# Gate-scaled one-hot matrices of the dense expert tiles: relu(gate - gate x distance) on ScalarE in place of a VectorE compare and a ScalarE scaling

## The chip, the cores and the metric

The kernel runs on one core of a Trainium2 chip. The metric is the device time of one execution in microseconds (us). A core has TensorE (PE in the profile; PEld is its weight load), VectorE (DVE), ScalarE (ACT), GpSimd (POOL) and SyncE (SP), each with its own queue of instructions that it works through in order, and DMA engines that all queues share.

## The reference

One layer of a decoder trunk on 1024 tokens of width 1024: a state-space branch, a dilated attention branch and a memory attention branch are merged and added to the residual, and then comes a retrieval of single-neuron experts. Only that last part matters here:

```
q = (hn @ w_query).reshape(b, s, 8, 2, 128)
sc = einsum('bshcd,hckd->bshck', q, sub_keys)
v1, i1 = top_k(sc[..., 0, :], 16);  v2, i2 = top_k(sc[..., 1, :], 16)
cand = v1[..., :, None] + v2[..., None, :]
cidx = i1[..., :, None] * 128 + i2[..., None, :]
top, pos = top_k(cand, 16);  idx = take(cidx, pos);  gate = softmax(top)
act = gelu(einsum('bld,blhkd->blhk', hn, expert_down[idx]))
out = einsum('blhk,blhkd->bld', gate * act, expert_up[idx])
```

There are 16384 experts; each token takes 8 x 16 = 128 of them, each with a gate.

## The kernel before

The sequence is worked through in two halves of four token tiles (128 tokens each). Of the eight tiles four (0, 1, 4, 5) gather their experts' rows by indirect DMA; the other four (2, 3, 6, 7, called DENSE) compute all 16384 experts and multiply each by its gate, which is zero for an expert that was not taken. For these a tile's gates have to be spread into a matrix "expert x token". `gates_of` does this: an expert number is `first * 128 + second`, and for each token a product of two one-hot matrices over its 128 slots, one from `second` (called `o2`) and one from `first` scaled by the gate (`og`), gives the 128x128 block of that token on TensorE.

`gates_of` begins with a set-up: it splits the expert numbers, transposes `first`, `second` and `gate` into one PSUM bank and copies them into `slots` (L1195). Then come 32 steps per tile, each for four tokens: a compare of `iota` with `second` (L1221), a compare of `iota` with `first` (L1222), both 128x512 on VectorE, four scalings of 128x128 on ScalarE (L1224), and, one step behind, `product()`: four matmuls of 128x128 (through the helper at L172, pinned in TensorE's program order) and a copy out of PSUM on ScalarE (L1207). After four steps a staging block is stored to `w_park` in device memory (L1210).

It runs in two places. For tiles 2 and 3 `early_gates` is a side job: `main()` steps it, by a counter of TensorE time, beside the attention and merging work of the second half; its one-hot matrices stand in the shared `work` buffers. For tiles 6 and 7 `dense` runs `gates()` together with `begin()`, which computes blocks of hidden activations (two 128x512 halves of weights loaded, cast on ScalarE at L244, the remainder on VectorE at L245, 24 matmuls, Gelu at L1266). There `hots` has room for four steps. Beside both run the side jobs of the gathered tiles: top-16 selection (`heads`), row products on VectorE (L1109, pinned) and the sums of rows on TensorE (L1154, pinned). After that the main loop of `dense` reads `w_park` back, so it begins when the last tile's blocks are stored.

The order of instructions on each engine is made when the program is built: by program order, readiness and the build's own cost estimates; pinned instructions keep their place, and weight casts in the mixing stages are moved ahead (`high_priority`).

Of the kernel before, what the change touches and what calls it, by code (L numbers as in the profile page):

```python
# [14 lines left out]
AF = mybir.ActivationFunctionType  # L15
ALU = mybir.AluOpType
# [86 lines left out]
def tile_hybrid_block(ctx: ExitStack, tc: tile.TileContext, keep_d, cst_d, vec_d, row_d, pos_d, xT_d, memT_d, w_in, w_mem_kv,  # L103
                      w_ssd_br, w_dil_br, w_mem_br, w_out, w_query, subk_d, down_d, up_d, downT_d, out):
    nc = tc.nc
# [44 lines left out]
    def gtiny(n, dt, tag, bufs):  # L150
        return new(gsmall, [P, n], dt, tag, bufs)[:, :n]
# [8 lines left out]
    def ps(tag=None):  # L160
        turn[0] += 1
        return bank(tag if tag and psums[tag][1] else "t" if turn[0] % 2 and psums["t"][1] else "s")
# [7 lines left out]
    def mm(o, lhsT, rhs, **kw):  # L170
        cost(o, 4 if rhs.dtype == F32 else 1)
        return nc.tensor.matmul(o, lhsT, rhs, **kw)  # L172

    def tr(o, x, i):
        cost(o, 2)
        nc.tensor.transpose(o, x, i)
# [6 lines left out]
    iota = keep[:, K_IOTA:K_IOTA + P]  # L183
# [914 lines left out]
    def pinned(ins):  # L1098

        tc.keep_in_program_order(ins)  # L1100
# [83 lines left out]
    def gates_of(d, expert, gate, alloc, ps, hot, stage_of):  # L1184

        t, slots = alloc(), alloc()
        ei = gtiny(P, I32, "ei", 1)
        nc.vector.tensor_copy(ei, expert)
        nc.vector.tensor_scalar(out=ei, in0=ei, scalar1=7, scalar2=None, op0=ALU.logical_shift_right)
        nc.vector.tensor_copy(t[:, 0:128], ei)  # L1190
        nc.vector.scalar_tensor_tensor(t[:, 128:256], t[:, 0:128], -128.0, expert, op0=ALU.mult, op1=ALU.add)
        tp = ps()
        for n, x in enumerate((t[:, 0:128], t[:, 128:256], gate)):
            tr(tp[:, n * P:(n + 1) * P], x, ident)
        nc.scalar.copy(slots[:, 0:384], tp[:, 0:384])  # L1195
        yield
        sl = slots[:, 0:384].rearrange("p (n t) -> p n t", n=3)
        iota4 = iota.unsqueeze(1).to_broadcast([P, 4, P])
        todo = []

        def product():
            (o2, og), stage, b, t4 = todo.pop(0)
            pw = ps()
            for tq in range(4):
                pinned(mm(pw[:, tq * P:(tq + 1) * P], o2[:, tq, :], og[:, tq, :], start=True, stop=True))
            for c0, n, part in stage:
                nc.scalar.copy(part[:, :, t4 * 4:t4 * 4 + 4], pw.rearrange("p (t c) -> p c t", t=4)[:, c0:c0 + n, :])  # L1207
            if t4 == WT // 4 - 1:
                for c0, n, part in stage:
                    nc.sync.dma_start(w_park[d * (P // WT) + b, :, c0:c0 + n, :], part)  # L1210

        for b in range(P // WT):
            stage = stage_of(b)
            for t4 in range(WT // 4):
                t0 = b * WT + t4 * 4

                def of(n):
                    return sl[:, n, t0:t0 + 4].unsqueeze(2).to_broadcast([P, 4, P])

                o2, og = (hot(n).rearrange("p (t c) -> p t c", t=4) for n in range(2))  # L1220
                nc.vector.tensor_tensor(out=o2, in0=iota4, in1=of(1), op=ALU.is_equal)  # L1221
                nc.vector.tensor_tensor(out=og, in0=iota4, in1=of(0), op=ALU.is_equal)  # L1222
                for tq in range(4):
                    nc.scalar.activation(out=og[:, tq, :], in_=og[:, tq, :], func=AF.Copy, scale=sl[:, 2, t0 + tq:t0 + tq + 1])  # L1224
                todo.append(((o2, og), stage, b, t4))
                if len(todo) == 2:
                    product()
                yield
        product()

    def dense(hn, dpool):
# [54 lines left out]
        def gates():  # L1286
            stages = new(dpool, [P, 2, P, WT], F32, "wbig", 2)
            hots = new(dpool, [P, 8, NW], F32, "wbig", 2)
            step = [0]

            def hot(n):
                step[0] += n == 0
                return hots[:, 2 * (step[0] % 4) + n, :]

            for d, tt in enumerate(DENSE):
                if tt >= NT:
                    while tt not in routed:
                        next(sides[-1][0])
                        yield
                    yield from gates_of(d, *routed[tt], dslab, big_ps, hot, lambda b: [(0, P, stages[:, b % 2])])  # L1300
# [92 lines left out]
    def early_gates():  # L1393
        def stage_of(b):
            return [(32 * k, 32, work().rearrange("p (c t) -> p c t", t=WT)) for k in range(4)]

        for d, tt in enumerate(DENSE):
            if tt < NT:
                while tt not in routed:
                    yield IDLE  # L1400
                for _ in gates_of(d, *routed[tt], work, ps, lambda n: work(), stage_of):
                    yield paces["gates"]
# [90 lines left out]
```

## Time and profile before

| what | value |
|---|---|
| runs of the kernel before | 4052.35 us median of 3 (4045.46 to 4067.32) |
| the profiled execution | 4053.3 us, span 4051.5 us |
| TensorE busy | 3770.0 us (93%) |
| VectorE busy | 2767.2 us (68%) |
| ScalarE busy | 1463.1 us (36%) |
| granted TensorE clock, mean | 0.960 |

The span is the time from the first to the last instruction of the profiled execution; the execution's own time is 1.8 us longer. Busy shares are over the whole span and mix stages with different limits. A granted clock of 1.0 is TensorE's full speed.

### The profile page before, as it was taken

The numbers are of one execution on the slowest core, as the hardware profiler recorded it, in microseconds if no ns is written. First come the engines' busy times: TensorE is split into PE (matmuls) and PEld (weight loads), VectorE is DVE, ScalarE is ACT, GpSimd is POOL, SyncE is SP. The second block draws the span as 40 slices with busy tenths as digits, with TensorE's granted clock in tenths as the row PEclk, the third lists the DMA queues.
The fourth block names the chain that finished last, engine by engine and source line by source line (L and its number), as shares of the span: only waits on it lengthen the run. The fifth ranks groups of instructions, "written<-read, shape, count | busy, mean of one in ns | idle before, by whom it ended". The sixth has DMA issues, their size and how long they took to land.

```text
span 4051.5 us, 54149 instructions
## 1 busy us (share of the span) xinstructions
PE 3770.0 (93%) x17838; PEld 2819.7 (70%) x17838; DVE 2767.2 (68%) x6987; ACT 1463.1 (36%) x3198; POOL 1424.6 (35%) x1257
## 2 busy tenths in 40 slices
PE   8989999999899998889888888999999999999997
PEld 5766888866676786667666676677777777777664
DVE  5763454558998768887768998976666666666432
ACT  3444344333333333445542564222223222222221
POOL 1210001101334433444345533444443344444444
PEclk9999999999999988989899999999999999999999
DMA  3233234443466757788788879989888888898888
GB/s 96 71 101 92 77 107 120 125 155 118 123 181 215 233 171 231 235 297 296 267 311 294 292 274 310 329 299 314 303 306 312 289 291 313 308 319 306 318 314 325
DMA packets 452826, 956.29 MB, mean 236 GB/s; under 512 B 44480, under 2 KB 173248, under 8 KB 450496
## 3 DMA queue, kind: packets, MB, share of 16 engines
q0 software_dynamic: 147456, 536.94, 38.0%
q1 hardware_dynamic: 305088, 415.90, 31.9%
q8 instruction: 140, 2.29, 0.2%
q14 instruction: 142, 1.16, 0.1%
HBM read 882.94 MB, written 69.73 MB: 235 GB/s over the span
## 4 chain that ended last, share of the span: by engine, by line
PE 31%; DMA 9%; DVE 8%; issue 4%; POOL 2%; ACT 1%; SPq 0%; POOLq 0%; another core or an unknown queue 0%; DVEq 0%; ACTq 0%
PE mm L172 15%; PE s L172 13%; DMA wraw<-in_downT_dram 4%; PE up L1154 4%; DVE wlo L245 1%; DMA wraw<-in_up_dram 1%; DVE rowd L1109 1%; DMA rowu<-in_up_dram,ids 1%; DMA rowd<-in_up_dram,ids 1%; POOL junk L1007 1%; POOL rowu L1168 1%; DVE wbig L1221 1%; DMA rowd<-in_down_dram,ids 1%; POOL rowd L1168 1%; DVE wbig L1222 1%
## 5 line engine op out<-in xcount | busy, mean ns | idle before, releaser
L245 DVE TENSOR_TENSOR wlo<-wraw,whi 128x512 fp32r<-128x512 f32 (+2 forms) x1002 | 714.0, 714 | 758.9 <-ACT whi L244 668.9
L244 ACT CAST whi<-wraw 128x512 fp32r<-128x512 f32 (+2 forms) x1002 | 612.7, 613 | 1704.7 <-PE mm L172 845.4
L1115 POOL DMA_INDIRECT rowd<-in_down_dram,ids x512 | 591.3, 1155 | 973.4 <-DVE act L1109 738.7
L172 PE MATMUL mm<-uslab,whi 128*128 128x512 f32 x2240 | 740.0, 409 | 6.2 <-DVE slab L427 5.9
L172 PE MATMUL s<-uslab,whi 128*128 128x512 f32 (+1 forms) x2080 | 667.2, 402 | 33.3 <-ACT whi L244 24.2
L172 PE MATMUL mm<-whi,coef 128*128 128x512 f32 x2048 | 677.4, 400 | 17.5 <-DVE acc L1345 10.7
L1109 DVE CUSTOM_DVE_ANT_0 rowd<-rowd,rowd 128x1024 f32<-128x1024 f32 x512 | 629.7, 1244 | 92.1 <-DMA rowd<-in_down_dram,ids 85.5
L1168 POOL DMA_INDIRECT rowu<-in_up_dram,ids x448 | 498.6, 1113 | 500.7 <-PE up L1154 380.0
L172 PEld LDWEIGHTS s<-uslab,whi 128*128 128x128 f32 (+1 forms) x2080 | 392.4, 191 | 161.2 <-ACT whi L244 34.2
L172 PEld LDWEIGHTS mm<-uslab,whi 128*128 128x128 f32 x2240 | 421.6, 193 | 99.1 <-issue 10.5
L172 PEld LDWEIGHTS mm<-whi,coef 128*128 128x128 f32 x2048 | 389.3, 190 | 142.8 <-issue 33.9
L172 PE MATMUL mm<-uslab,wlo 128*128 128x512 f32 x1120 | 454.0, 406 | 16.7 <-DVE wlo L245 16.6
L172 PE MATMUL s<-uslab,wlo 128*128 128x512 f32 (+1 forms) x1040 | 416.4, 400 | 11.1 <-DVE wlo L245 9.4
L172 PE MATMUL mm<-wlo,coef 128*128 128x512 f32 x1024 | 408.4, 399 | 2.2 <-DVE wlo L245 2.2
L172 PE MATMUL mm<-slab,whi 128*128 128x512 f32 x768 | 258.2, 415 | 18.3 <-DVE slab L245 6.2
L172 PEld LDWEIGHTS mm<-uslab,wlo 128*128 128x128 f32 x1120 | 215.4, 193 | 70.8 <-DVE wlo L245 21.1
L172 PEld LDWEIGHTS s<-uslab,wlo 128*128 128x128 f32 (+1 forms) x1040 | 198.3, 191 | 64.7 <-DVE wlo L245 17.3
L1154 PE MATMUL up<-rowu,one_col 128*32 128x512 f32 x1792 | 225.7, 611 | 18.8 <-DMA rowu<-in_up_dram,ids 18.8
L172 PE MATMUL mm<-whi,uslab 128*128 128x512 f32 (+1 forms) x768 | 240.4, 394 | 0.0
L1007 POOL TENSOR_TENSOR junk<-junk,code 128x800 f32<-128x800 f32 x64 | 129.6, 2025 | 294.7 <-DVE junk L1005 273.7
L172 PEld LDWEIGHTS mm<-wlo,coef 128*128 128x128 f32 x1024 | 194.9, 190 | 49.3 <-DVE wlo L245 4.5
L172 PEld LDWEIGHTS mm<-slab,whi 128*128 128x128 f32 x768 | 147.3, 196 | 56.5 <-DVE slab L245 8.9
(315 smaller groups left out, 5077.0 us busy)
## 6 DMA issues: line engine op xcount, KB each, us to landing
wraw<-in_downT_dram SPq DMA_DIRECT2D x256, 256.0 KB
wraw<-in_up_dram SPq DMA_DIRECT2D x256, 256.0 KB
wraw<-in_w_in_dram SPq DMA_DIRECT2D x152, 256.0 KB
wbig<-w_park SPq DMA_DIRECT2D x16, 2048.0 KB
wraw<-in_w_in_dram SPq DMA_DIRECT2D x160, 128.0 KB
slab<-y_park SPq DMA_DIRECT2D x64, 256.0 KB
wraw<-in_w_query_dram SPq DMA_DIRECT2D x64, 256.0 KB
w_park<-work SPq DMA_DIRECT2D x64, 256.0 KB
```

The lines of the kernel that those rows point to most:

```text
L172: return nc.tensor.matmul(o, lhsT, rhs, **kw)
L244: nc.scalar.copy(hi, src)
L245: nc.vector.tensor_tensor(out=lo, in0=src, in1=hi.bitcast(F32), op=ALU.subtract)
L1007: nc.gpsimd.tensor_tensor(out=junk, in0=junk, in1=d3[:, h, :].unsqueeze(1).to_broadcast([P, 16, NCAND]), op=ALU.mult)
L1109: pinned(nc.vector.tensor_tensor_reduce(out=r, in0=r, in1=hn, scale=1.0, scalar=0.0, op0=ALU.mult, op1=ALU.add, accum_out=act[:, j:j + 1]))
L1115: nc.gpsimd.indirect_dma_start(out=r, out_offset=None, in_=down_d, in_offset=bass.IndirectOffsetOnAxis(ap=ids[:, j:j + 1], axis=0))
L1154: pinned(nc.tensor.matmul(up[32 * q:32 * q + 32, hh * 512:(hh + 1) * 512], z[:, q, 31 - n:63 - n], four[q][:, hh * 512:(hh + 1) * 512], st ...
L1168: nc.gpsimd.indirect_dma_start(out=r, out_offset=None, in_=up_d, in_offset=bass.IndirectOffsetOnAxis(ap=ids[:, 128 + t:129 + t], axis=0))
L1221: nc.vector.tensor_tensor(out=o2, in0=iota4, in1=of(1), op=ALU.is_equal)
L1222: nc.vector.tensor_tensor(out=og, in0=iota4, in1=of(0), op=ALU.is_equal)
```

## The change

In the set-up the transposed gates are also written with their sign turned. In each step the compare of `iota` with `first` goes. In its place ScalarE makes, for each of the four tokens, the distance |first - iota| and then relu(gate - gate x distance): at distance 0 that is the gate, at any distance from 1 on it is 0. The compare for `o2`, the products and the stores stay.

```diff
         nc.scalar.copy(slots[:, 0:384], tp[:, 0:384])
+        nc.scalar.activation(out=slots[:, 384:512], in_=tp[:, 256:384], func=AF.Copy, scale=-1.0)
         yield
-        sl = slots[:, 0:384].rearrange("p (n t) -> p n t", n=3)
+        sl = slots[:, 0:512].rearrange("p (n t) -> p n t", n=4)
...
                 nc.vector.tensor_tensor(out=o2, in0=iota4, in1=of(1), op=ALU.is_equal)
-                nc.vector.tensor_tensor(out=og, in0=iota4, in1=of(0), op=ALU.is_equal)
                 for tq in range(4):
-                    nc.scalar.activation(out=og[:, tq, :], in_=og[:, tq, :], func=AF.Copy, scale=sl[:, 2, t0 + tq:t0 + tq + 1])
+                    first, gate_t, neg_t = (sl[:, n, t0 + tq:t0 + tq + 1] for n in (0, 2, 3))
+                    nc.scalar.activation(out=og[:, tq, :], in_=iota, func=AF.Abs, scale=-1.0, bias=first)
+                    nc.scalar.activation(out=og[:, tq, :], in_=og[:, tq, :], func=AF.Relu, scale=neg_t, bias=gate_t)
```

## Rows read from the trace of the kernel before

**Rows 1.** The page's engine totals: busy us, share of the span, instructions.
```profile
PE 3770.0 (93%) x17838; PEld 2819.7 (70%) x17838; DVE 2767.2 (68%) x6987; ACT 1463.1 (36%) x3198; POOL 1424.6 (35%) x1257
```

**Rows 2.** Late stage by stretch: us, busy us (instructions) per engine, clock, DMA.
```profile
2275.00:2390.00 115.00, 105.08 (x598) 83.45 (x598) 107.87 (x333) 73.25 (x193) 53.57 (x41) 0.96 0.89 320
2390.00:2460.00 70.00, 60.16 (x346) 49.40 (x346) 65.30 (x226) 60.19 (x174) 23.41 (x12) 0.95 0.64 232
...
2305.00:2320.00 15.00, 15.00 (x97) 11.89 (x96) 14.45 (x35) 13.27 (x32) 7.03 (x7) 1.00 0.85 315
2425.00:2440.00 15.00, 13.86 (x89) 11.28 (x88) 15.00 (x45) 14.78 (x46) 1.54 (x1) 0.91 0.27 92
```

**Rows 3.** Chain of waits from 2282 to 2460 us, shares by line.
```profile
by line: DVE wbig L1221 14.5%; DVE wbig L1222 12.7%; PE s L172 12.3%; PE mm L172 7.5%; POOL junk L1007 7.4%; DMA rowu<-in_up_dram,ids 5.9%; issue 5.8%; DVE rowd L1109 4.5%; DVE wlo L245 4.3%; PE up L1154 3.2%; DVE junk L1005 3.0%; ACT wbig 
```

**Rows 4.** Waits in the late stage: waiter, releaser, us in total, times, longest.
```profile
ACT wbig L1224 <- DVE wbig L1222: 37.4, 16, 7.1
...
PE mm L172 <- ACT wbig L1224: 18.1, 29, 5.0
```

**Rows 5.** ScalarE in order of time, late stage: start us, us, instruction.
```profile
2426.28 1.28 ACT L1224 ACTIVATE wbig<-wbig,coef 128x128 f32<-128x128 f32 x4
2427.46 0.57 ACT L1207 COPY wbig<-mm 128x512 f32<-128x512 f32 x1
2427.93 1.28 ACT L1224 ACTIVATE wbig<-wbig,coef 128x128 f32<-128x128 f32 x4
```

**Rows 6.** Early stage, and the stretch behind the late one, by engine.
```profile
1690.00:2080.00 390.00, 344.68 (x1756) 253.23 (x1752) 298.61 (x627) 211.19 (x673) 178.49 (x149) 0.93 0.82 293
...
2460.00:4051.00 1591.00, 1511.77 (x7078) 1094.96 (x7076) 988.52 (x1870) 417.47 (x701) 710.71 (x634) 0.98 0.89 311
```

**Rows 7.** Waits in the early stage.
```profile
ACT work L1224 <- DVE work L1222: 55.6, 24, 8.9
...
PEld s L172 <- ACT work L1224: 20.6, 16, 4.2
```

**Rows 8.** Groups by line and shape, VectorE's compare L1222 in the late stage: busy us, mean ns | idle before.
```profile
L1222 DVE TENSOR_TENSOR wbig<-keep,coef 128x512 f32<-128x512 f32 x64 | 43.6, 682 | 0.0
```

**Rows 9.** Groups by line and shape on ScalarE, with none, one and two column operands.
```profile
L532 ACT ACTIVATE slab<-slab,cw 128x512 f32<-128x512 f32 x32 | 26.1, 815 | 1.6 <-POOL slab L527 0.4
L537 ACT ACTIVATE slab<-slab 128x512 f32<-128x512 f32 x32 | 20.2, 633 | 10.8 <-DVE slab L534 9.9
L713 ACT ACTIVATE work<-work,tiny 128x128 f32<-128x128 f32 x36 | 14.2, 398 | 13.3 <-DVE tiny L707 12.0 <-DVE tiny L732 1.3
L1075 ACT ACTIVATE gate<-gate 128x128 f32<-128x128 f32 x8 | 2.5, 309 | 8.4 <-DVE gate L1074 8.3
```

**Rows 10.** The same view, the scalings of the late stage.
```profile
L1224 ACT ACTIVATE wbig<-wbig,coef 128x128 f32<-128x128 f32 x256 | 82.5, 399 | 41.1 <-DVE wbig L1222 37.4 <-DVE posf L1002 2.3 <-DVE wbig L1221 1.0
```

**Rows 11.** ScalarE in order of time: an instruction that reads the one before.
```profile
320.60 0.59 ACT L853 COPY slab<-mm 128x512 f32<-128x512 f32 x1 [0.33 <-PE mm L172]
321.21 0.63 ACT L855 ACTIVATE slab<-slab 128x512 f32<-128x512 f32 x1
```

**Rows 12.** VectorE in order of time: two dependent chains.
```profile
2305.77 0.28 DVE L965 MAX8 vals<-sc 128x8 f32<-128x128 f32 x1
...
2306.04 0.19 DVE L967 MATCH_REPLACE8 cand<-top,cand 128x50 f32<-128x50 f32 x1
...
2306.22 0.28 DVE L966 FIND_INDEX8 idxs<-vals,sc 128x8 uint32<-128x128 f32 x1
```

**Rows 13.** TensorE in order of time, one step of the late stage.
```profile
2443.57 1.37 PE L172 MATMUL mm<-wbig 128*128 128x128 f32 x8 [0.28 <-ACT wbig L1224]
```

**Rows 14.** Groups on ScalarE: table loads, Gelus of the late stage, absolute values.
```profile
L1266 ACT ACTIVATE g<-s 128x512 f32<-128x512 f32 x13 | 7.6, 588 | 2.0 <-PE s L172 2.0
...
L1266 ACT ACT_TABLE_LOAD x1 | 1.3, 1283 | 0.0
...
L492 ACT ACTIVATE tiny<-tiny 128x64 f32<-128x64 f32 x2 | 0.5, 256 | 9.7 <-DVE tiny L489 9.7
```

## The prediction

> **What bounds the kernel now.** I read the page's engine totals first [rows 1]: over the whole span TensorE is the busiest engine (93%), VectorE has 68% and ScalarE 36%. An average like that says nothing on a change that sits in two short stages, so next came the stages. The gate-building steps of tiles 2 and 3 run from 1690 to 2080 us beside the second half's attention work (the early stage), those of tiles 6 and 7 from 2275 to 2460 us (the late stage); elsewhere the changed lines do not run. Each stage has 64 steps. In the late stage [rows 2] VectorE is busy for 107.87 of 115 us and 65.30 of 70, ScalarE for 73.25 and 60.19, TensorE for 105.08 and 60.16. The reader should see that two engines are near full at once: VectorE throughout, ScalarE in the second part. The slices of 15 us show where each has room: ScalarE 13.27 us in the fullest slice of the first part, 14.78 in the second.
>
> The chain of waits inside the late stage confirms VectorE's part: the two compares have 14.5% and 12.7% of it [rows 3]. ScalarE sat idle for 37.4 us until the compare that is to go, and TensorE for 18.1 us until ScalarE's scaling [rows 4]. The instructions in order of time show the other regime [rows 5]: from about 2425 us on four scalings take 1.28 us, the copy out of PSUM follows, and the next four start 1.65 us after the last four, with nothing between. TensorE waits 0.28 us in each such step. There ScalarE alone sets the pace.
>
> In the early stage ScalarE has 211.19 of 390 us, VectorE 298.61, TensorE 344.68 [rows 6]; no engine is full, and what costs time is who waits in order: ScalarE 55.6 us for the compare, the weight loads of the products 20.6 us for ScalarE [rows 7].
>
> **What the change removes.** 128 compares of 128x512 on VectorE, 64 in each stage, 43.6 us in the late one [rows 8]; and with them the waits of ScalarE for that compare.
>
> **What it adds.** In each step the four scalings become four absolute values and four Relus, eight ScalarE instructions for four.
>
> *Price of an absolute value.* It has one operand in a per-partition column (the bias). A 128x128 instruction with no column took 0.309 us, with one 0.398 [rows 9]; the present scaling takes 0.399 [rows 10]. So 0.398. Four independent ones take 1.28 us together, so one follows another after (1.28 - 0.398)/3 = 0.294, and instructions overlap by 0.104.
>
> *Price of a Relu.* It has two columns, scale and bias. At 128x512 the step from none to two is 0.815 - 0.633 = 0.182 [rows 9]. On 0.309 that makes 0.491, or 0.387 when it overlaps its neighbour.
>
> *Does the pair overlap?* The Relu reads what the absolute value has just written. The trace has such a pair on ScalarE: the squaring at L855 starts at 321.21, the copy that feeds it began at 320.60 and took 0.59, so it starts 0.02 us after the copy's end, with no overlap [rows 11]. Written strictly in the code's order, a pair costs 0.398 + 0.02 + 0.387 = 0.805 us. But where two dependent chains were free to go, the instruction order alternated them: on VectorE the top-16 chain of the candidates and that of the scores stand one after the other in turn [rows 12]. I take it that absolute values of the next token are put between likewise, because this is the same case (a dependent successor and an independent one); then a pair costs 0.294 + 0.387 = 0.681. I keep 0.805 as the upper bound. Below, nothing excludes less than 0.681 except that each instruction would have to be shorter than every one of its kind in the trace.
>
> *Sum per step.* Before 4 x 0.294 = 1.18, after 4 x 0.681 = 2.72: 1.55 us more, 99.1 us more ScalarE work in each stage. The one extra scaling in each tile's set-up (4 in all, some 0.3 us each) is hidden behind the transposes' stage; uncovered it is 1.2 us.
>
> **Late stage.** First part: 73.25 + 32 x 1.55 = 122.9 us of ScalarE work for a stretch of 115, so 8 us over even if ScalarE never rests; at the 88% of its fullest slice it would be 139 us, 24 over. I take 14, nearer to the lower, because the wait for the compare goes. Second part: 60.19 + 49.6 = 109.8 us for a stretch of 70; at the 98.5% of the slice from 2425 us 111.5, so 42 over. Together +56. Nothing hides it: the main loop's first load of gates needs the last store of the last tile, and the TensorE work between (the hidden blocks) is fixed. TensorE gets idle time in each step, which may lower its granted clock; with 1.37 us of products in a step of some 3.2 us [rows 5, 13], twice the time for them would still fit.
>
> **Early stage.** 211.19 + 99.1 = 310 us in 390, so the work fits; the cost is only in waits. An isolated step takes as long as before: two compares and four scalings were about 0.60 + 0.68 + 1.28 = 2.56 us from first to last, now ScalarE alone needs 2.72 and the remaining compare runs beside it. In bursts the products wait longer, and behind the pairs stand the casts of the weight blocks, for which TensorE waits. Lower bound: all of the products' 20.6 us of waiting goes with the compare, -20. Upper: it grows with ScalarE's work, 20.6 x 2.72/1.18 = 47.5, +27. I take +10, nearer to the upper, since ScalarE's work grows for certain and the freed VectorE is not full here.
>
> **Sum.** The profiled execution took 4053.3 us (span 4051.5); that is 1 us above the median of the runs. 4053.3 + 56 + 10 = 4119.
>
> A rule speaks against the change: the Trainium skill, page "ScalarE: Activation LUTs", section "Rules for kernel authors", says to put Relu, max, add and multiply on VectorE. This trace agrees for this shape: 128x512 compared in 0.68 us on VectorE [rows 8], against 2.72 us on ScalarE for what replaces it and the scaling.
>
> **The rivals.**
>
> *VectorE was the bound (faster).* For it: VectorE's share of the late stage, and the chain that runs through the compare. If ScalarE kept up, the late stage would lose at most 43.6 us and the early one 20: 3990. Against it: ScalarE's free time in the late stage is 115 - 73.25 + 70 - 60.19 = 51.6 us for 256 pairs. The rival decides only if a pair costs at most 0.294 + 51.6/256 = 0.495 us; that is about one two-column instruction alone. Chance 3%.
>
> *Absorbed (no change).* The hidden blocks' matrix work moves ahead of products that wait, the late stage grows by some 30 and the early stage gives 20 back: about 4063. For it: the order is not fixed for the hidden blocks' matmuls. Against it: ScalarE's own work overflows by 48 us whatever TensorE does. 8%.
>
> *Pairs in strict order (slower still).* 4 x (0.805 - 0.294) = 2.04 us per step, 131 per stage: late 133.4 + 131 - 185 = 79, with the same idle share 88; early 18. 4159. 18%.
>
> *Table loads.* If Relu were not in the table that Gelu needs, each of the late stage's 13 Gelus would be flanked by two loads of 1.283 us [rows 14], +33: 4152. For it: no Relu stands in the trace. Against it: the absolute value at L492 ran twice, and the view lists no load at that line [rows 14]. 3%. The Trainium skill, same page, section "Table sets: the hidden batching unit", says that cheap functions such as Relu, copy and abs are in every set; by it there is no load, and the sum stays at 4119.
>
> *Early stage goes wrong.* Weight casts queue behind bursts of pairs beyond the bound above, the stage costs +45 or more: 4155 and up. 6%.
>
> **How the numbers follow.** The forecast itself has 62%. Its own spread is 4080 (late +47, early -20) to 4138 (late +58, early +27). Leaving out the faster rival, the absorbed one and the far end of the slower ones, the range is 4075 to 4175. The measurement can tell about 0.5% (20 us) from no change. Faster 0.03; within 0.5%, 0.08; slower 0.89.
>
> **What would show it.** Right: the late stage ends some 50 us later, ScalarE near full from its start to its end, a step of about 3.2 us in its last part, TensorE waiting there for the Relus; VectorE's share of it down to about 130 of 240 us; absolute values in pairs ahead of their Relus. The stretch behind it (1591 us before) keeps its length. Wrong: a pair near 0.5 us or near 0.8; a table load beside each Gelu; the early stage longer than 420 us; or the stretch behind the late stage shorter, which would mean that gathers ran ahead in the added time.

## The result, and the profile after

The changed kernel takes 4153.84 us (median of 4 runs, 4150.09 to 4169.31); the kernel before took 4048.96 us (median of 4). The ratio is 1.0268, with a 95% interval of 1.0246 to 1.0291: 105 us slower, where 66 us were forecast. The direction and the range held; the term for the late stage was too small, and the forecast's own spread (4080 to 4138) did not reach so far.

The page's engine totals of the changed kernel (busy us, share of the span, instructions) answer to [rows 1]:

```profile
PE 3812.8 (92%) x17838; PEld 2841.2 (68%) x17838; DVE 2702.0 (65%) x6859; ACT 1654.8 (40%) x3714; POOL 1395.0 (34%) x1257
```

VectorE lost 65 us of work and ScalarE gained 192, close to twice the 99.1 us worked out for each stage. The profiled execution took 4152.15 us, 98.9 more than that of before. The windows of the changed kernel (us, then busy us and instructions of TensorE, its weight loads, VectorE, ScalarE and GpSimd, granted clock, DMA share, GB/s) answer to [rows 2, 6] and say where:

```profile
1680.00:2100.00 420.00, 359.89 (x1796) 262.64 (x1789) 267.65 (x568) 306.61 (x935) 178.28 (x153) 0.90 0.81 284
2280.00:2450.00 170.00, 122.92 (x604) 92.52 (x603) 155.05 (x660) 126.25 (x328) 70.33 (x53) 0.84 0.68 239
2450.00:2555.00 105.00, 82.03 (x318) 60.09 (x317) 38.24 (x111) 104.54 (x294) 14.23 (x11) 0.61 0.34 128
2560.00:4150.00 1590.00, 1511.86 (x7083) 1096.24 (x7081) 937.32 (x1587) 414.80 (x698) 679.04 (x623) 0.98 0.89 309
2490.00:2505.00 15.00, 11.42 (x40) 8.76 (x39) 3.46 (x5) 15.00 (x44) 0.00 (x0) 0.50 0.17 71
```

The stretch behind the late stage kept its length (1590 us, before 1591) and the late stage begins only 5 us later; nearly all of the loss lies in the late stage. Cut by its own instructions (from the set-up copy L1195 of tile 6 to that of tile 7, and from there to the last store to `w_park`; the remainder of the span in the last column), all kernels of this study compare so, in us of one profiled execution each (one execution can lie some 18 us from its kernel's median: that of "changed, tiles 4 and 5 held" took 4141.09, the median is 4159.38):

| kernel | late stage begins | tile 6's part | tile 7's part | late stage | behind it |
|---|---|---|---|---|---|
| before | 2275.3 | 117.5 | 62.7 | 180.2 | 1596.0 |
| changed | 2280.1 | 171.3 | 103.8 | 275.1 | 1595.2 |
| early stage only | 2278.0 | 118.2 | 62.6 | 180.8 | 1605.2 |
| late stage only | 2271.4 | 169.4 | 103.7 | 273.1 | 1584.4 |
| Relu alone | 2283.8 | 125.2 | 90.8 | 216.0 | 1582.4 |
| one operation on VectorE | 2267.1 | 129.7 | 73.6 | 203.3 | 1602.1 |
| changed, selections held | 2300.6 | 143.8 | 103.7 | 247.5 | 1612.1 |
| Relu alone, selections held | 2283.7 | 107.6 | 68.7 | 176.3 | 1628.4 |
| before, selections held | 2284.9 | 112.1 | 67.6 | 179.7 | 1601.5 |
| changed, weight casts ahead | 2278.7 | 148.9 | 116.5 | 265.4 | 1599.4 |
| changed, tiles 4 and 5 held | 2277.8 | 151.0 | 103.7 | 254.7 | 1606.8 |
| Relu alone, tiles 4 and 5 held | 2274.7 | 113.8 | 69.2 | 183.0 | 1609.3 |
| before, tiles 4 and 5 held | 2263.5 | 114.4 | 68.6 | 183.0 | 1615.3 |
| fourth token on VectorE | 2270.2 | 114.6 | 75.6 | 190.2 | 1625.1 |

Tile 7's part grew by 41 us (forecast 42). Tile 6's part grew by 54 (forecast 14).

**Tile 7's part is as forecast.** ScalarE in order of time, changed kernel (start us, us, instruction, count), answers to [rows 5]:

```profile
2487.02 0.73 ACT L1225 ACTIVATE wbig<-keep,coef 128x128 f32<-128x128 f32 x2
2487.62 0.91 ACT L1226 ACTIVATE wbig<-wbig,coef 128x128 f32<-128x128 f32 x2
2488.39 0.72 ACT L1225 ACTIVATE wbig<-keep,coef 128x128 f32<-128x128 f32 x2
2488.97 0.91 ACT L1226 ACTIVATE wbig<-wbig,coef 128x128 f32<-128x128 f32 x2
2489.74 0.61 ACT L1208 COPY wbig<-mm 128x512 f32<-128x512 f32 x1
```

Absolute values stand in pairs ahead of their two Relus, so here no Relu directly follows the instruction that it reads. From one copy (2486.56 in the same view) to the next is 3.18 us, for a step that took 1.65 us before [rows 5]; ScalarE is busy for all 15 us of the slice at 2490, with VectorE at 3.46. TensorE in order of time answers to [rows 13]:

```profile
2488.20 2.58 PE L172 MATMUL mm<-wbig 128*128 128x128 f32 x8 [0.62 <-ACT wbig L1226]
2491.38 2.58 PE L172 MATMUL mm<-wbig 128*128 128x128 f32 x8 [0.61 <-ACT wbig L1226]
```

Its granted clock there is 0.50, the 1.2 GHz level, and a step's products take 2.58 us instead of 1.37. This costs nothing: 2.58 fits in a step of 3.18, and TensorE still waits for the Relu each time.

Groups by line and shape on ScalarE, late stage (busy us, mean ns | idle before, releasers), answer to [rows 10, 14]:

```profile
L1226 ACT ACTIVATE wbig<-wbig,coef 128x128 f32<-128x128 f32 x256 | 115.9, 514 | 0.0
L1225 ACT ACTIVATE wbig<-keep,coef 128x128 f32<-128x128 f32 x256 | 92.0, 423 | 0.0
...
L1268 ACT ACTIVATE g<-s 128x512 f32<-128x512 f32 x12 | 7.1, 594 | 28.1 <-PE s L172 28.0
...
L1268 ACT ACT_TABLE_LOAD x2 | 2.6, 1283 | 0.0
```

The prices were 0.398 and 0.491 us in the forecast; the groups say 0.423 and 0.514. Lines 1225 and 1226 have no table load, and only two stand beside the twelve Gelus, so the table rival is out.

**Tile 6's part is not.** ScalarE is busy for 126.25 of 170 us: its work is what was forecast (122.9), but it rests for 44 us, 28 of them ahead of Gelus. The waits of the changed kernel in that part (waiter, releaser, us in total, times, longest) answer to [rows 4]:

```profile
PEld s L172 <- DVE wlo L245: 28.4, 10, 5.8
ACT g L1268 <- PE s L172: 28.0, 8, 8.0
...
PEld s L172 <- ACT whi L244: 17.8, 7, 3.9
```

The same view of the kernel before over its whole late stage has next to nothing of this; there the remainder of the weight cast (`wlo`, VectorE) let TensorE wait once:

```profile
ACT g L1266 <- PE s L172: 2.0, 2, 1.8
...
PEld s L172 <- DVE wlo L245: 0.2, 1, 0.2
```

So a chain of waits has formed: Gelu on ScalarE waits for the hidden block on TensorE, that waits for the remainder on VectorE, and that for its place behind other work on VectorE. One case of it, in order of time, changed kernel, first VectorE:

```profile
2420.54 1.28 DVE L1222 TENSOR_TENSOR wbig<-keep,coef 128x512 f32<-128x512 f32 x2
...
2422.12 0.68 DVE L1222 TENSOR_TENSOR wbig<-keep,coef 128x512 f32<-128x512 f32 x1
...
2424.91 0.29 DVE L965 MAX8 vals<-sc 128x8 f32<-128x128 f32 x1 [1.79 <-DMA sc<-sc_park]
2425.12 0.31 DVE L965 MAX8 top<-cand 128x8 f32<-128x50 f32 x2
2425.34 1.27 DVE L245 TENSOR_TENSOR wlo<-wraw,whi 128x512 fp32r<-128x512 f32 x2
```

then TensorE and, separately, ScalarE:

```profile
2426.07 0.80 PE L172 MATMUL s<-uslab,wlo 128*128 128x512 f32 x1 [5.37 <-DVE wlo L245]
```

```profile
2419.29 1.14 ACT L244 CAST whi<-wraw 128x512 fp32r<-128x512 f32 x2
...
2433.85 0.60 ACT L1268 ACTIVATE g<-s 128x512 f32<-128x512 f32 x1 [8.00 <-PE s L172]
```

ScalarE had the two casts done at 2420.43. VectorE began their remainder only at 2425.34. Of the 4.9 us between, three compares of the gates took 2 us (L1222 in this kernel, `iota` with `second`), and nearly all of the rest went to steps of top-16 selections, one of which (L965) waited 1.79 us for its scores from memory. TensorE lost 5.37 us. ScalarE then lost 8.00, which holds TensorE's work on the late block as well. That selection belongs to a gathered tile and has nothing to do with the gates.

Such selections were moved here. The selection for one head (eight to a tile) ends in a reduction at L1008; the groups by line between 2275 and 2460 us count them, first in the kernel before, then in the changed one:

```profile
L1008 DVE TENSOR_REDUCE expert<-junk 128x16 f32<-128x800 f32 x9 | 8.8, 981 | 8.6 <-POOL junk L1007 8.6
```

```profile
L1008 DVE TENSOR_REDUCE expert<-junk x16: 960/975/987, 2297.0 to 2452.4; 128x16 f32<-128x800 f32 x16
```

Nine became sixteen. VectorE lost 43.6 us of compares in this stage and yet is busy for 155 of 170 us; it has correspondingly less behind the stage (937 us, before 988.52 [rows 6]). The build put other work in the place that came free. Whether that, or ScalarE's work alone, made the 54 us was the question for the experiments.

### The profile page after: what moved, and what is told of

Same layout as the page of the kernel before. It is cut to its first block, busy times and chain, and to the rows that moved or that the text cites. A ratio compares the mean times of both kernels' runs of the same rounds, so it can differ in the third digit from the quotient of the medians.

```text
span 4150.4 us, 54474 instructions
## 1 busy us (share of the span) xinstructions
PE 3812.8 (92%) x17838; PEld 2841.2 (68%) x17838; DVE 2702.0 (65%) x6859; ACT 1654.8 (40%) x3714; POOL 1395.0 (34%) x1257
## 4 chain that ended last, share of the span: by engine, by line
PE 35%; DMA 11%; DVE 6%; ACT 4%; issue 3%; POOL 2%; POOLq 0%; SPq 0%; DVEq 0%; ACTq 0%
PE mm L172 17%; PE s L172 14%; PE up L1154 4%; DMA wraw<-in_downT_dram 4%; DMA wraw<-in_up_dram 1%; ACT wbig L1226 1%; DMA rowd<-in_up_dram,ids 1%; DVE wlo L245 1%; DMA rowd<-in_down_dram,ids 1%; DVE rowd L1109 1%; ACT wbig L1225 1%; DMA rowu<-in_up_dram,ids 1%; POOL junk L1007 1%; DMA sc<-sc_park 1%; POOL rowd L1168 1%
## 5 line engine op out<-in xcount | busy, mean ns | idle before, releaser
L1115 POOL DMA_INDIRECT rowd<-in_down_dram,ids x512 | 579.0, 1131 | 1005.4 <-DVE act L1109 773.5
L172 PE MATMUL s<-uslab,whi 128*128 128x512 f32 (+1 forms) x2080 | 677.3, 407 | 45.3 <-ACT whi L244 39.6
L1168 POOL DMA_INDIRECT rowu<-in_up_dram,ids x448 | 485.5, 1084 | 602.7 <-PE up L1154 481.3
L172 PEld LDWEIGHTS mm<-slab,whi 128*128 128x128 f32 x768 | 146.6, 195 | 79.1 <-DVE slab L245 17.8
```

Source lines behind the costliest of these rows:

```text
L1115: nc.gpsimd.indirect_dma_start(out=r, out_offset=None, in_=down_d, in_offset=bass.IndirectOffsetOnAxis(ap=ids[:, j:j + 1], axis=0))
L1168: nc.gpsimd.indirect_dma_start(out=r, out_offset=None, in_=up_d, in_offset=bass.IndirectOffsetOnAxis(ap=ids[:, 128 + t:129 + t], axis=0))
```

## The experiments

Ratios are to the kernel before, run on the same chip.

**1. Each stage by itself.** The new form only for tiles 2 and 3, or only for 6 and 7; elsewhere the compare and the scaling stay.

```diff
+                if not (d < 2):
+                    nc.vector.tensor_tensor(out=og, in0=iota4, in1=of(0), op=ALU.is_equal)
...
+                    if not (d < 2):
+                        nc.scalar.activation(out=og[:, tq, :], in_=og[:, tq, :], func=AF.Copy, scale=gate_t)
+                        continue
```

The other kernel has `if not (d >= 2)` in both places.

> Only tiles 2 and 3 build their gates in the new way; tiles 6 and 7 keep the compare and the scaling. Theory: in the changed kernel's trace the late stage begins 5 us later than before and ends 99 us later, so the early stage should cost next to nothing: 0 to +10 us against the kernel before, 4050 to 4062. Rival (the early stage delays work that only shows later): +30 us or more.

> Only tiles 6 and 7 build their gates in the new way. Theory: the whole loss is here, +90 to +105 us against the kernel before, 4140 to 4155. Rival (the loss needs both stages): +70 us or less.

Measured: early alone 1.0047 (1.0033 to 1.0061), +19 us; late alone 1.0228 (1.0201 to 1.0256), +92, as its theory had it. They add up to 111, the changed kernel's 105 within the intervals, so the stages can be explained one by one. The early figure lies between its theory and its rival. In its one profile the late stage begins 2.7 us later and the stretch behind lasts 9 longer; where the early stage's loss arises is thus not settled. What the rows do show of that stage is which wait grew. Waits of the changed kernel there, answering to [rows 7]:

```profile
DVE wlo L245 <- ACT whi L244: 29.4, 18, 10.2
...
PEld s L172 <- ACT work L1226: 11.8, 9, 5.0
```

and of the kernel before:

```profile
DVE wlo L245 <- ACT whi L244: 17.4, 14, 2.5
```

The products wait less than before (11.8 us against 20.6 [rows 7]); VectorE waits longer for the weight casts on ScalarE (29.4 us against 17.4).

**2. Is the second ScalarE instruction the cost, or the freed VectorE?** The absolute value is left out, the compare too, so ScalarE has as many instructions as before.

```diff
-                    first, gate_t, neg_t = (sl[:, n, t0 + tq:t0 + tq + 1] for n in (0, 2, 3))
-                    nc.scalar.activation(out=og[:, tq, :], in_=iota, func=AF.Abs, scale=-1.0, bias=first)
-                    nc.scalar.activation(out=og[:, tq, :], in_=og[:, tq, :], func=AF.Relu, scale=neg_t, bias=gate_t)
+                    gate_t, neg_t = (sl[:, n, t0 + tq:t0 + tq + 1] for n in (2, 3))
+                    nc.scalar.activation(out=og[:, tq, :], in_=iota, func=AF.Relu, scale=neg_t, bias=gate_t)
```

> The absolute value is left out: one Relu with two column operands per token, made straight from the iota row, so the gate matrices hold other values than they should; the compare on VectorE stays gone. ScalarE's step is 4 x 0.387 + 0.46 = 2.0 us against 1.65 before, +24 us of work in the late stage, where it had 51.6 us free. Theory (the loss is ScalarE's overflow, and the compare's removal is worth something): between -40 and 0 us against the kernel before, 4010 to 4050. Rival (the freed VectorE time fills with other work, and the loss comes from that, not from the second ScalarE instruction): +40 us or more.

Measured 1.0111 (1.0084 to 1.0139), +45 us: my theory fell, and the rival's figure came. The compare's 43.6 us are gone, ScalarE has only some 25 us more (158 in the two windows below, before 133 [rows 2]), and the late stage is 36 us longer than before. Its windows, tile 6's part and tile 7's:

```profile
2284.00:2409.00 125.00, 108.90 (x603) 85.67 (x602) 111.36 (x425) 90.23 (x203) 56.65 (x42) 0.92 0.82 295
2409.00:2500.00 91.00, 59.75 (x316) 48.55 (x315) 74.81 (x333) 68.12 (x165) 30.23 (x20) 0.79 0.52 184
```

VectorE's busy time did not fall: 186 us in this stage, 173 before [rows 2].

**3. The other engine.** On the kernel before, compare and scaling become one VectorE instruction per token.

```diff
-                nc.vector.tensor_tensor(out=og, in0=iota4, in1=of(0), op=ALU.is_equal)
                 for tq in range(4):
-                    nc.scalar.activation(out=og[:, tq, :], in_=og[:, tq, :], func=AF.Copy, scale=sl[:, 2, t0 + tq:t0 + tq + 1])
+                    first, gate_t = (sl[:, n, t0 + tq:t0 + tq + 1] for n in (0, 2))
+                    nc.vector.tensor_scalar(out=og[:, tq, :], in0=iota, scalar1=first, scalar2=gate_t, op0=ALU.is_equal, op1=ALU.mult)
```

> The compare and the four scalings become four compare-and-multiply instructions on VectorE (128x128, expert number and gate as column operands); ScalarE builds nothing of the matrix. In the late stage ScalarE falls from 130 to some 50 us of 180, VectorE changes by 4 x (0.15 to 0.25) - 0.60 us per step, 0 to +26 us. Theory (the late stage's end is set by whichever of the two engines is full, and ScalarE is no longer one): -30 to +10 us, 4020 to 4060. Rival (VectorE was the true limit before): +15 us or more.

Measured 1.0101 (1.0076 to 1.0127), +39 us: the theory fell here too, and the rival's figure (VectorE was the true limit) came. The group of the new instruction in its late stage, and the window of tile 7's part:

```profile
L1224 DVE TENSOR_SCALAR wbig<-keep,coef 128x128 f32<-128x128 f32 x256 | 84.6, 386 | 0.0
```

```profile
2397.00:2470.00 73.00, 54.60 (x313) 43.56 (x312) 73.00 (x288) 20.38 (x36) 12.54 (x10) 0.86 0.52 191
```

84.6 us on VectorE take the place of 43.6 [rows 8] (0.330 us for one, above the 0.15 to 0.25 expected), and tile 7's part has VectorE busy throughout. For this shape VectorE is the better place of the two: the late stage is 203.3 us against 275.1. The rule of the Trainium skill, page "ScalarE: Activation LUTs", section "Rules for kernel authors", to use VectorE and not ScalarE for Relu, max, min, add and multiply, holds in that comparison; but the kernel before, which splits the pair over both engines, is shorter than either (180.2).

**4. Selections held in place.** The first instruction of each half-selection keeps its place in VectorE's program order; the same edit on the changed kernel, on Relu alone, and on the kernel before as control.

```diff
-        nc.vector.max(out=v[:, 0:8], in_=x)
+        first_max = nc.vector.max(out=v[:, 0:8], in_=x)
+        if up_pool:
+            tc.keep_in_program_order(first_max)
```

> The changed kernel, with the first maximum of every top-16 selection held in its traced place on VectorE (from the second half on), so that no selection moves ahead into the late stage: 8 half selections stand there as in the kernel before, against 18 in the changed kernel. New theory: about 50 us of the loss is ScalarE's overflow and some 40 us is selection work that fills the freed VectorE time and holds up compares and casts; +50 to +75 us against the kernel before. Rival (the moved selections are harmless, ScalarE alone sets the loss): +95 to +110 us.

> One Relu per token without the absolute value, as in the earlier run (other values in the gate matrices), with the selections held in place. There +45 us, although ScalarE's work fits. New theory: the selections were the cause, -20 to +10 us against the kernel before. Rival: again +35 to +50 us.

> The kernel before with the selections held in place: the control. Both theories: -10 to +10 us; a larger gain or loss would have to be taken off the two other runs.

Measured 1.0277 (1.025 to 1.0304), 1.0078 (1.0058 to 1.0098) and 1.0068 (1.0043 to 1.0093). All three are above what their theories said. The control is not neutral: holding costs 26 us by itself, with the late stage starting later, so only differences to it can be read. Relu alone is then 8 us above its control, within their intervals (45 us when free), and the changed kernel 89 (105 when free). In the late stage, Relu alone is no longer above its control (176.3, 179.7). Its windows:

```profile
2284.00:2391.00 107.00, 98.78 (x577) 78.32 (x578) 85.71 (x295) 85.32 (x196) 43.69 (x35) 0.96 0.84 307
2391.00:2460.00 69.00, 57.25 (x318) 43.56 (x317) 48.49 (x173) 66.85 (x165) 17.32 (x13) 0.95 0.56 206
```

Here the compare is really gone from VectorE (134 us in 176), and still nothing is gained: TensorE fills 92% of the first part and ScalarE, with 21 us more work than in the control (152 against 131), 97% of the second. And with the selections held in both, one more ScalarE instruction per token takes the late stage from 176.3 to 247.5: 71 us for 256 absolute values, which at 0.294 us each are 75 us.

**5. Held for tiles 4 and 5 only**, the selections that the late stage contains, to spare the control its loss.

```diff
-        nc.vector.max(out=v[:, 0:8], in_=x)
+        first_max = nc.vector.max(out=v[:, 0:8], in_=x)
+        if held:
+            tc.keep_in_program_order(first_max)
...
-            for _ in two_heads(qd, sc, *found[tt]):
+            for _ in two_heads(qd, sc, *found[tt], tt in (4, 5)):
```

> The changed kernel, with only the selections of tiles 4 and 5 held in their traced place, so that the stage before the late one is left alone (holding all of them lengthened it). Theory: the late stage takes 245 to 250 us from the first set-up to the last store, as with all held (275 in the changed kernel, 180 before), and this time the total shows it: +65 to +85 us against the kernel before. Rival (the work held back costs as much behind the late stage): +95 us or more.

> One Relu per token without the absolute value (other values in the gate matrices), selections of tiles 4 and 5 held. Theory: late stage 175 to 185 us, total -10 to +15 us against the kernel before (+45 with the selections free). Rival: +30 us or more.

> The kernel before with the selections of tiles 4 and 5 held: the control. 8 half selections stand in the late stage either way. Theory: -10 to +10 us. Rival (holding costs by itself): +20 us or more, to be taken off the other two.

Measured 1.0281 (1.0258 to 1.0303), 1.0068 (1.0044 to 1.0093) and, the control, 1.003 (1.0016 to 1.0044). Above the control: changed 101 us, the rival's figure; Relu alone 15. The late stages repeat experiment 4 (254.7 and 183.0, again 72 us apart). In the changed kernel so held the reductions between 2275 and 2460 us (L1010 there) are eight, not sixteen:

```profile
L1010 DVE TENSOR_REDUCE expert<-junk x8: 968/986/987, 2295.0 to 2446.6; 128x16 f32<-128x800 f32 x8
```

Windows of it, tile 6's part, then of the control:

```profile
2278.00:2429.00 151.00, 117.00 (x606) 88.99 (x605) 99.15 (x333) 124.94 (x328) 45.91 (x40) 0.86 0.71 251
```

```profile
2263.00:2378.00 115.00, 105.19 (x608) 83.98 (x609) 107.19 (x336) 76.63 (x199) 50.11 (x40) 0.97 0.90 324
```

Tile 6's part falls from 171.3 to 151.0 us (143.8 in experiment 4), with VectorE at 99 of 151 instead of 155 of 170. It stays 37 us above its control. Its waits in that part:

```profile
PEld s L172 <- ACT whi L244: 17.9, 7, 3.9
...
PEld s L172 <- DVE wlo L245: 13.0, 6, 4.8
...
ACT g L1270 <- PE s L172: 7.2, 7, 2.9
```

The wait for remainders fell from 28.4 to 13.0 us and that of the Gelus from 28.0 to 7.2; the wait for the casts on ScalarE is what it was (17.8, now 17.9).

But the total gets nothing back: my theory's figure for it failed in both experiments. The selections that are held have to run behind the stage (VectorE has 993 us there, 937 in the changed kernel), and that stretch is 12 us longer in the profile.

**6. Weight casts ahead of the pairs** in the changed kernel.

```diff
-                split(raw, hi, lo)
+                with tc.high_priority(offset=URGENT):
+                    split(raw, hi, lo)
```

> The changed kernel with the weight casts of the hidden blocks moved ahead in the order of both engines. Rival to the new theory: the idle 28 us of ScalarE before the Gelus come from casts that queue behind the pairs, then +50 to +75 us against the kernel before. New theory: the compares still stand behind the selections, at most 20 us come back, +85 to +110 us.

Measured 1.0244 (1.0219 to 1.0269), 4147.24 us. Tile 6's part falls to 148.9 us and tile 7's part rises to 116.5, so the stage gets 10 back, as expected; the total is within the intervals of the changed kernel's. The casts' place behind the pairs is thus a part of tile 6's loss: its wait for remainders is nearly gone.

```profile
PEld s L172 <- DVE wlo L245: 1.4, 2, 0.9
```

What tile 7's part lost is not ScalarE work: ScalarE has 104.34 us in it, as without the edit (104.54), but rests for 12. A wait of TensorE in this part, and the instructions behind it on VectorE and ScalarE:

```profile
PE mm L172 <- DVE wbig L1222: 16.2, 1, 16.2
```

```profile
2442.39 2.48 DVE L1222 TENSOR_TENSOR wbig<-keep,coef 128x512 f32<-128x512 f32 x4
```

```profile
2445.30 0.59 ACT L1208 COPY wbig<-mm 128x512 f32<-128x512 f32 x1 [11.21 <-PE mm L172]
```

From 2428.4 to 2442.4 VectorE works on nothing but steps of selections; tile 7's first compares stand behind them, TensorE waits 16.2 us for these and ScalarE 11.2 for the product. So the selections hold up the stage in this kernel too, at another place.

**7. One token of four on VectorE**, only in tile 7's part, on the control of experiment 5, to see whether a finer split than the present one pays.

```diff
+                whole = 3 if d == 3 else 4
...
+                    if tq < whole:
+                        nc.scalar.activation(out=og[:, tq, :], in_=og[:, tq, :], func=AF.Copy, scale=gate_t)
+                    else:
+                        nc.vector.tensor_scalar(out=og[:, tq, :], in0=iota, scalar1=first, scalar2=gate_t, op0=ALU.is_equal, op1=ALU.mult)
```

> The control with one more edit, against the change's direction: in tile 7 the fourth token of a step is compared and scaled by one VectorE instruction, so ScalarE's step falls from 1.65 to about 1.35 us and VectorE's rises by about 0.12. Theory (ScalarE sets the pace in tile 7's part): its 62.7 us fall to 52 to 58, the total by 5 to 10 us against the control. Rival (VectorE, busy 58.7 of 62 us there, sets it just as much): 0 to +4 us.

Measured 1.0071 (1.0053 to 1.0089) against the control's 1.003: 21 us slower, and both expectations too low. Tile 7's part, this kernel:

```profile
2385.00:2460.00 75.00, 57.05 (x313) 47.27 (x312) 68.89 (x238) 48.16 (x132) 18.91 (x13) 0.80 0.56 202
```

ScalarE fell to 48 us, VectorE rose to 69 of 75 and the part is 7 us longer than the control's 68.6. No kernel of this study beats the kernel before.

## Why the prediction was right, and where it was short

*What bounds the kernel.* Right: both engines are near full in the late stage. Putting more on VectorE loses (experiments 3 and 7), and so does putting more on ScalarE. The faster rival is out by the result and by its own condition: it needed a pair at 0.495 us or less, and in tile 7's part two pairs take 1.37 us (2487.02 to 2488.39). Relu alone with the selections held takes the compare off VectorE and gains nothing, but it also adds 21 us to ScalarE; what the compare's removal is worth with ScalarE's work unchanged was not tried.

*Prices and order.* Right. The instructions cost 0.423 and 0.514 us with their neighbours overlapping, the pairs alternate, one pair follows the last after 0.685 us (0.681 forecast), a step takes 3.18 us (3.2 forecast). "Pairs in strict order" forecast a total (4159) close to the measured one, but its mechanism is not there: its step would be 1.65 + 2.04 = 3.69 us. So it was luck that the range held: the forecast's own bounds at their worst (24 + 42 in the late stage, 27 in the early one) end at 4146, below the measured time, and the range reached past it for the sake of slower rivals whose mechanisms did not come.

*Sum per step.* Right: ScalarE did 230.8 us of work in the late stage; the forecast has 122.9 + 109.8 = 232.7.

*Late stage, second part.* Right: +42 forecast, +41 measured. ScalarE alone sets the pace, so work and time are the same.

*Late stage, first part.* This step failed: "I take 14, nearer to the lower, because the wait for the compare goes." Measured +54. The work was right; the share of time in which ScalarE could do it was not. I bounded it by 100% and by the 88% of its fullest slice. But the fullest slice is the best that the stretch did, no lower end; the whole stretch had 73.25 of 115, 64% [rows 2]. With that, 122.9 us of work would take 193 us, and the measured 171.3 (126.25 of 170, 74%) lies between. The wait for the compare did go; others came in its place, as the chain of waits above shows, and "ScalarE near full from its start to its end" did not come. Of the 54 us, holding the selections takes off 20 (tiles 4 and 5) or 28 (all), so the selections that the build moved into VectorE's free time are that part of the stage's loss. Against their controls 37 and 32 us stay. Of these some 10 are work that doesn't fit (124.94 in a stretch of 115); for the others the waits for casts (17.9) and remainders (13.0) that are left with tiles 4 and 5 held are the likely cause. That is argued and not shown: the casts were not moved with the selections held.

*Early stage.* +10 forecast between -20 and +27; +19 by experiment 1. The direction and the bounds held. The reason was half right: the waits for the casts grew, but the products, whose waits made the upper bound, waited less. From its first set-up copy to its last store the stage took 411 us (1683.3 to 2094.3), before 386, so the sign set at 420 did not come.

*Hidden or not.* "Nothing hides it" held: the stretch behind the stage kept its length. VectorE's busy time in the late stage was forecast at about 130 us and was 193, the plainest sign in the profile of what the forecast had left out.

*What stays open.* Holding the selections lengthens other stretches, in the kernel before too (+26 and +12 us), by a way that I did not follow. So what the moved selections cost in total is known only by two estimates each, with an uncertainty of 10 to 15 us: 30 and 37 us of Relu alone, 4 and 16 of the changed kernel. And the early stage's 19 us were measured, not located. In the table the late stage of the new form begins 5 to 16 us after that of its like (2280.1 and 2275.3; 2300.6 and 2284.9; 2277.8 and 2263.5), with the new early stage alone 3 us, so a part may arise ahead of it.

## What to carry to other kernels

Compare the work that an edit adds to an engine with that engine's free time in the very stage: 51.6 us were free on ScalarE, 99 came, and no relief of another engine changed the sign in any run here. For the size, take the busy share that the whole stretch had as one bound, not its best slice, because an engine that exchanges results with others keeps waiting for them. And where the order is made at build time, ask what will fill the time that comes free: here it was selections, which then stood ahead of the remainders and compares that TensorE needed.

## What was not expected of the hardware

TensorE's granted clock stayed at 0.50 in slices where it was busy for 11.4 of 15 us, in groups of eight 128x128 products with waits of 0.61 us between them; in the same part of the kernel before, with waits of 0.28 us, it was 0.91 [rows 2, 13]; no run changed these waits alone. And VectorE's comparing and multiplying with two column operands cost 84.6 / 256 = 0.330 us for a 128x128 tile, so that four of them take twice as long as one 128x512 compare with no multiplication (0.682 us [rows 8]).
